# A decoder trunk on one core: the shared filter sum of the convolution moves to ScalarE and GpSimd, and the memory matrices are made in three passes of split float32

## The chip, the core and the metric

The kernel runs on one core of one Trainium2 chip. A core has a matrix engine (TensorE, PE in the profile, with its weight loads shown apart as PEld), a vector engine (VectorE, DVE), an engine for activation functions (ScalarE, ACT), a general engine (GpSimd, POOL), and a queue engine that here issues the transfers (SyncE, SP). Each works through its own list of instructions in order and waits on semaphores for the others. The metric is the device time of one execution in microseconds (us), the median of several executions.

## The reference

The model is a trunk of two layers on 1024 tokens of width 1024, all in float32. The first layer's token mixer is a gated convolution, the second's is forgetting attention. Each layer then attends to 256 memory tokens and ends in an MLP.

```python
def conformer_conv(h, w_pw1, b_pw1, w_dw, b_dw, ln_g, ln_b, w_pw2, b_pw2):
    u = h @ w_pw1 + b_pw1
    a, gate = jnp.split(u, 2, axis=-1)
    u = a * jax.nn.sigmoid(gate)
    u = depthwise_conv(u, w_dw, width 31, causal) + b_dw
    u = jax.nn.silu(layernorm(u, ln_g, ln_b))
    return u @ w_pw2 + b_pw2

def memory_cross_attention(h, mem_n, w_q, w_k, w_v, w_o):
    q, k, v = h @ w_q, mem_n @ w_k, mem_n @ w_v        # 4 heads of 256
    p = softmax(q k^T / sqrt(256))
    return (p v) @ w_o
```

Only the convolution and the preparation for the cross-attention matter here. `mem_n` is the root-mean-square norm of the memory, with a gain per layer.

## The kernel before

Activations lie transposed: 8 chunks of 128 features on the partitions, 1024 tokens along the free side, in two halves of 512 (`X`, `HALVES`). A product in full precision is made of three fast passes: an operand is split into a high part (`act.copy` into the type float32r) and a low part (the rest, `low`, a subtraction), and `passes` multiplies low by high, high by low and high by high. `product` runs these passes into one PSUM bank. An operand that comes as one plain float32 tile is multiplied in one float32 product instead; the profile shows each such product as two matmul instructions.

**The convolution layer** (`conv_layer`). For each chunk m, `gated_unit` makes both halves of `u`: two products of 24 passes each per half, a sigmoid on ScalarE, and one VectorE instruction (L370) that writes `u`. `convolve` then runs the filter of 31 taps over `u`. It uses a trick that halves the work of even and odd output positions: tokens are kept as an even row and an odd row, and

- `both` is a sum over the odd row with the sums of neighbouring taps (`sums`), shared by the even and the odd outputs: 16 steps (L396, then L400 fifteen times);
- `d0` and `d1` are differences of the two rows (L393, L394);
- the even outputs are `both` plus 16 taps on `d0`, the odd outputs `both` plus 15 taps on `d1` (L408). Two accumulators, the two halves of `X`, are built at once; in the built program their instructions alternate.

L354 adds each chunk's result to a running sum for the layer norm. When all 8 chunks are done, `layer_norm` normalizes the halves (L314, L183, L317, L318), and `linear` multiplies by `pw2` (384 passes, results written by L324).

**The memory preparation** (`memory_matrices`) does not depend on the tokens. For each layer and each of 4 heads it makes the keys `kt` and values `vt` of the memory, and from them two matrices that go to DRAM for the attention (`mqk`, `mvo`). It is a generator: four steps to a head, 32 in all, and `conv_layer` calls some of them between its own pieces (`next(prep)`), so that TensorE has work while VectorE runs the filter. In plain float32 it needs 128 products with 256 columns for keys and values a layer, 64 for `mqk`, and 32 with 512 columns for `mvo`.

The order of the instructions on each engine is set when the program is built, by the scheduler of the Tile framework: it works by the order of the code, by priorities and by its own estimate of what is ready. On the chip nothing overtakes. The pool `nrm` has a ring of four buffers under the tag `t`, which squares, the filter's intermediate tiles and others take in the order of the code; whoever takes a buffer waits until the fourth one before has been read.

Of the kernel before, what the change touches and what calls it, by code (L numbers as in the profile page):

```python
# [12 lines left out]
F32 = mybir.dt.float32  # L13
F32R = mybir.dt.float32r
# [72 lines left out]
def trunk(ctx, tc, a, out):  # L87
# [16 lines left out]
    def col(name, i):  # L104
        return par[:, COLS[name] + i : COLS[name] + i + 1]
# [80 lines left out]
    def add_squares(acc, ch):  # L186

        sq = nrm.tile([P, HALF], F32, name="sq", tag="t", bufs=4)
        act.activation(sq, ch, AF.Square)
        if acc is None:  # L190
            return sq
        dve.tensor_tensor(acc, acc, sq, op=ALU.add)
        return acc
# [98 lines left out]

    def conv_layer(pm, prep):
        with tc.tile_pool(name="conv", bufs=2) as cp:
# [44 lines left out]
            for m in range(NCH):  # L339
                if m:  # L340
                    u = padded()
                    for sl in HALVES:
                        gated_unit(pm, cp, m, ahead, hs, u[:, :, PAD // 2 :], sl)
                if m + 1 < NCH:
                    ahead = gate_weights(m + 1)
                for _ in range(2):
                    next(prep, None)

                convolve(cp, m, u, pairs[:, m])
                for s, sl in enumerate(HALVES):  # L350
                    if m == 0:
                        act.copy(acc[s], X[:, m, sl])
                    else:
                        dve.tensor_tensor(acc[s], acc[s], X[:, m, sl], op=ALU.add)  # L354
# [30 lines left out]

    def convolve(cp, m, u, sums):


        n, k = S // 2, TAPS // 2
        even, odd = u[:, 0, :], u[:, 1, :]  # L390
        d0 = cp.tile([P, n + k], F32, name="d0")
        d1 = cp.tile([P, n + k - 1], F32, name="d1")
        dve.tensor_tensor(d0, even[:, : n + k], odd[:, : n + k], op=ALU.subtract)  # L393
        dve.tensor_tensor(d1, even[:, 1 : n + k], odd[:, : n + k - 1], op=ALU.subtract)  # L394
        both = cp.tile([P, n], F32, name="both")
        dve.tensor_scalar(  # L396
            both, odd[:, :n], sums[:, 0:1], col("dw_b", m), op0=ALU.mult, op1=ALU.add
        )
        for j in range(1, k + 1):
            dve.scalar_tensor_tensor(  # L400
                both, odd[:, j : j + n], sums[:, j : j + 1], both, op0=ALU.mult, op1=ALU.add
            )
        out = [X[:, m, sl] for sl in HALVES]
        for s, d, taps in ((0, d0, k + 1), (1, d1, k)):
            y = both
            for j in range(taps):
                w = col("dw_w", m * TAPS + 2 * j + s)
                dve.scalar_tensor_tensor(  # L408
                    out[s], d[:, j : j + n], w, y, op0=ALU.mult, op1=ALU.add
                )  # L410
                y = out[s]

# [20 lines left out]
    def memory_matrices(pp, pq, layer):  # L433
# [3 lines left out]

        def get(src):
            raw = pp.tile([P, NCH, P], F32, name="praw", bufs=3)
            nc.sync.dma_start(raw, src)  # L440
            return raw

        mem = pp.tile([P, NCH, MEM], F32, name="mem", bufs=1)
        nc.sync.dma_start(mem, a["memT"])
        if layer == 0:
            r = inverse_rms([mem[:, c, :] for c in range(NCH)], RMS_EPS)
            rt = const.tile([P, MEM // P], F32, name="mem_r")
            rs = const.tile([P, MEM], F32, name="mem_rs")
            mem_r.extend((rt, rs))
        for c in range(NCH):  # L450
            act.activation(mem[:, c, :], mem[:, c, :], AF.Copy, scale=col(f"src{layer}", c))
        for h in range(MEM_HEADS):
            kv = []
            for w, n in ((wk, "kt"), (wv, "vt")):
                t = bank(pq).rearrange("p (c m) -> p c m", c=2)
                for c in range(2):
                    x = get(w[2 * h + c])
                    product(t[:, c, :], [((x[:, k, :],), (mem[:, k, :],)) for k in range(NCH)])
                o = pp.tile([P, 2, MEM], F32, name=n, bufs=1)
                if w is wk:  # L460
# [3 lines left out]
                    rb = mem_r[1].unsqueeze(1).to_broadcast([P, 2, MEM])  # L464
                    with tc.high_priority(offset=SMALL_FIRST):
                        dve.tensor_tensor(o, t, rb, op=ALU.mult)
                else:
                    act.copy(o, t)
                kv.append(o)
                yield  # L470
            kt, vt = kv
            for j in range(2):

                x = get(wq[h, j])
                for g in range(2):
                    t = bank(pq).rearrange("p (f m) -> p f m", f=2)
                    o = pp.tile([P, 4, P], F32, name="o").rearrange("p (f b) n -> p f (b n)", f=2)
                    for f in range(2):
                        product(t[:, f, :], [
                            ((x[:, 4 * c + 2 * g + f, :],), (kt[:, c, :],)) for c in range(2)  # L480
                        ])
# [6 lines left out]
            for j in range(2):  # L488

                x = get(wo[h, j])  # L490
                for mc in range(2):
                    t = bank(pq)
                    product(t, [
                        (
                            (vt[:, c, mc * P : (mc + 1) * P],),
                            (x[:, 4 * c : 4 * c + 4, :].rearrange("p b n -> p (b n)"),),
                        )
# [864 lines left out]

    with prep_pools(4) as pools, banks(2) as pm:
        conv_layer(pm, chain(*(memory_matrices(*pools, l) for l in range(2))))
    sums = mem_attention(0)
# [80 lines left out]
```

## Time and profile before

| | us |
|---|---|
| median of 3 runs | 2822.2 (2816.68 to 2823.24) |
| the profiled execution's own time | 2825.31 |
| its span, first to last instruction | 2823.3 |
| convolution layer: up to the last write of L324 | 526 |
| of it, the eight filters | 77 to 388 |

The page lists busy time of each engine over the whole span. Lines are those of the kernel before. A duration in it is that of one instruction with its pipeline; where instructions follow each other closely, the distance between two starts is shorter than the duration, and a group's busy time (its union) divided by its count shows that distance. A matmul of 512 columns for example is listed with 391 ns, and 5424 of them fill 1242.4 us, 229 ns each.

### The profile page before, as it was taken

How to read it: one execution, taken by the hardware profiler on the slowest of the kernel's cores; microseconds unless marked ns; L12 is line 12 of the kernel's file. 1: busy time of each engine (PE TensorE's matmuls, PEld its weight loads, DVE VectorE, ACT ScalarE, POOL GpSimd, SP SyncE). 2: the span in 40 equal slices, each digit the busy share in tenths (PEclk: the TensorE clock that was granted, in tenths of full speed). 3: DMA queues.
4: the chain of work that ended last, by engine and by line, in shares of the span. 5: the costliest groups of instructions: out<-in, count | busy, mean ns of one | idle time of the engine just before them, and what ended most of it. 6: DMA issues, size and time to landing. Idle time of an engine off the chain costs nothing.

```text
span 2823.3 us, 36214 instructions
## 1 busy us (share of the span) xinstructions
PE 2740.8 (97%) x12968; PEld 2261.3 (80%) x12968; DVE 2030.9 (72%) x3358; ACT 1278.3 (45%) x2293; POOL 703.1 (25%) x473
## 2 busy tenths in 40 slices
PE   8999999999999999999899999989999999989998
PEld 6777777888888877888688888878888788878886
DVE  5999984555776576777788888875546855577776
ACT  5212143433555553333466666673423655543332
POOL 0000000000065625774000000000000365525773
PEclk9999999999999999999899999999999999999999
DMA  6334364322165585652222221243213455655651
GB/s 219 120 119 135 114 206 124 101 90 70 65 230 177 178 309 187 227 199 89 69 68 70 57 65 55 69 136 98 94 64 105 149 176 190 218 208 197 227 201 61
DMA packets 165428, 390.68 MB, mean 138 GB/s; under 512 B 17264, under 2 KB 46192, under 8 KB 164992
## 3 DMA queue, kind: packets, MB, share of 16 engines
q1 hardware_dynamic: 165248, 388.37, 40.9%
q8 instruction: 102, 1.67, 0.2%
q14 instruction: 78, 0.64, 0.1%
HBM read 270.79 MB, written 113.31 MB: 136 GB/s over the span
## 4 chain that ended last, share of the span: by engine, by line
PE 74%; DVE 12%; ACT 5%; DMA 5%; issue 3%; POOL 1%; SPq 0%; DVEq 0%; POOLq 0%; ACTq 0%
PE mm L1070 34%; PE mm L269 29%; PE mm L1255 5%; DVE w L148 2%; DVE op L148 2%; DVE x L408 1%; PE mm L1341 1%; DVE x L1310 1%; DMA ua<-x 1%; ACT x L1315 1%; PE mm L1353 1%; PE mm L1354 1%; DVE both L400 1%; DVE wl L148 1%; ACT pth L151 1%
## 5 line engine op out<-in xcount | busy, mean ns | idle before, releaser
L1070 PE MATMUL mm<-op,w 128*128 128x512 f32 x5424 | 1242.4, 391 | 24.5 <-ACT m L955 8.7
L1070 PEld LDWEIGHTS mm<-op,w 128*128 128x128 f32 x5424 | 1020.5, 189 | 243.2 <-ACT m L955 9.6
L269 PE MATMUL mm<-op,wh 128*128 128x512 f32 x1056 | 330.5, 394 | 4.2 <-DVE op L148 4.2
L148 DVE TENSOR_TENSOR w<-r,w 128x512 fp32r<-128x512 f32 x264 | 262.6, 998 | 30.5 <-ACT w L653 30.5
L653 ACT CAST w<-r 128x512 fp32r<-128x512 f32 x264 | 163.3, 622 | 262.0 <-PE mm L1070 233.2
L269 PEld LDWEIGHTS mm<-op,wh 128*128 128x128 f32 x1056 | 200.2, 190 | 48.5 <-DVE op L148 6.5
L1255 PE MATMUL mm<-op,wh 128*128 128x512 f32 x736 | 231.4, 396 | 0.0
L148 DVE TENSOR_TENSOR w<-t,w 128x512 fp32r<-128x512 f32 x180 | 178.2, 1005 | 63.2 <-ACT w L653 63.1
L269 PE MATMUL mm<-op,wl 128*128 128x512 f32 x528 | 210.5, 400 | 7.1 <-DVE wl L148 6.2
L207 POOL TENSOR_TENSOR r<-v,mhalf 128x4 f32<-128x4 f32 (+1 forms) x15 | 16.8, 1117 | 741.0 <-DVE v L205 741.0
L647 POOL TENSOR_TENSOR t<-r,t 128x512 f32<-128x512 f32 x104 | 174.9, 1681 | 91.4 <-DVE w L148 54.2
L653 ACT CAST w<-t 128x512 fp32r<-128x512 f32 x180 | 112.0, 622 | 169.8 <-PE mm L1070 140.6
L151 ACT CAST wh<-raw 128x1024 fp32r<-128x1024 f32 x96 | 100.7, 1050 | 193.8 <-PE mm L269 97.5
L865 POOL TENSOR_TENSOR x<-x,x 128x512 f32<-128x512 f32 x112 | 160.2, 1455 | 112.6 <-ACT x L878 101.6
L967 DVE TENSOR_TENSOR x<-mm,x 128x512 f32<-128x512 f32 x160 | 109.5, 684 | 91.1 <-PE mm L1070 73.7
L1255 PEld LDWEIGHTS mm<-op,wh 128*128 128x128 f32 x736 | 139.2, 189 | 26.7
L269 PE MATMUL mm<-op,xsh 128*128 128x512 f32 x512 | 158.0, 393 | 0.0
L1255 PE MATMUL mm<-op,wl 128*128 128x512 f32 x368 | 155.0, 421 | 1.9 <-ACT q L1275 1.9
L151 ACT CAST pth<-mm 128x512 fp32r<-128x512 f32 (+1 forms) x224 | 105.9, 495 | 108.5 <-PE mm L556 80.8
L408 DVE SCALAR_TENSOR_TENSOR x<-d,par,x 128x512 f32<-128x512 f32 x232 | 154.5, 746 | 0.0
L647 POOL TENSOR_TENSOR t<-r,r 128x512 f32<-128x512 f32 x52 | 80.2, 1542 | 295.1 <-DMA r<-in_ff_w 191.0
L1315 ACT ACTIVATE x<-x,nb 128x128 f32<-128x128 f32 (+7 forms) x128 | 99.5, 778 | 109.3 <-DVE nb L1313 100.0
(188 smaller groups left out, 4689.6 us busy)
## 6 DMA issues: line engine op xcount, KB each, us to landing
r<-in_ff_w SPq DMA_DIRECT2D x128, 512.0 KB, 4.0
op<-ua SPq DMA_DIRECT2D x80, 512.0 KB, 6.8
us<-x SPq DMA_DIRECT2D x128, 256.0 KB, 2.9
op<-us SPq DMA_DIRECT2D x64, 512.0 KB, 5.6
raw<-mvo SPq DMA_DIRECT2D x32, 512.0 KB, 3.4
ua<-ul SPq DMA_DIRECT2D x64, 256.0 KB, 2.2
ua<-uh SPq DMA_DIRECT2D x60, 256.0 KB, 2.3
raw<-in_pw SPq DMA_DIRECT2D x24, 512.0 KB, 4.7
```

The lines of the kernel that those rows point to most:

```text
L148: dve.tensor_tensor(lo, src, hi.bitcast(F32), op=ALU.subtract)
L151: act.copy(hi, src)
L269: pe.matmul(out_ps, x, y, start=i == 0, stop=i == len(terms) - 1)
L400: dve.scalar_tensor_tensor(both, odd[:, j : j + n], sums[:, j : j + 1], both, op0=ALU.mult, op1=ALU.add)
L408: dve.scalar_tensor_tensor(out[s], d[:, j : j + n], w, y, op0=ALU.mult, op1=ALU.add)
L647: (dve if g in (2, 3, UP, UP + 1) else pool).tensor_tensor(t, raws[g, x], raws[g, y], op=ALU.subtract)
L653: act.copy(highs[n][0], raws[steps[n][:2]])
L865: eng.tensor_tensor(u[g, x], y1, y2, op=op_)
L967: dve.tensor_tensor(v, sums[key], v, op=ALU.add)
L1070: pe.matmul(sums[key], y, z, start=first and i == 0, stop=n == last_of[key] and i == len(terms) - 1, skip_group_check=True,)
L1255: pe.matmul(t, x, y, start=n == 0, stop=n == len(terms) - 1)
L1315: act.activation(x[:, :n], x[:, :n], AF.Exp, bias=nb, accum_out=rs)
```

## The change

`both` is no longer made on VectorE. ScalarE multiplies the odd row by each tap (`tap`, L397 of the changed kernel; the first step, L394, writes `both` and adds the bias), and GpSimd adds the 15 products to `both`, one after the other (L398). VectorE keeps the differences (now L401, L402) and the 31 taps (L409), which now accumulate in one PSUM bank, `acc`, instead of in the two halves of `X`: first all of `d0`, then all of `d1`. `d0` and `d1` have one buffer each instead of two.

The memory preparation takes split operands. Weights come in halves of 4 chunks; ScalarE makes the high part (`ph`, L448), GpSimd the low part (`pl`, L449), three buffers each. The memory, the keys and the values are split too (`memh`, `meml`, `kth`, `ktl`, `vth`, `vtl`), their low parts on VectorE (L462, L148). The keys' full form is now a tile of the ring `t`. The preparation's PSUM pool goes from 4 banks to 3.

```diff
+        both = cp.tile([P, n], F32, name="both")
+        act.activation(both, odd[:, :n], AF.Identity, scale=sums[:, 0:1], bias=col("dw_b", m))
+        for j in range(1, k + 1):
+            t = nrm.tile([P, HALF], F32, name="tap", tag="t", bufs=4)
+            act.activation(t, odd[:, j : j + n], AF.Copy, scale=sums[:, j : j + 1])
+            pool.tensor_tensor(both, both, t, op=ALU.add)
+        d0 = cp.tile([P, n + k], F32, name="d0", bufs=1)
+        d1 = cp.tile([P, n + k - 1], F32, name="d1", bufs=1)
...
-        both = cp.tile([P, n], F32, name="both")
-        dve.tensor_scalar(
-            both, odd[:, :n], sums[:, 0:1], col("dw_b", m), op0=ALU.mult, op1=ALU.add
-        )
-        for j in range(1, k + 1):
-            dve.scalar_tensor_tensor(
-                both, odd[:, j : j + n], sums[:, j : j + 1], both, op0=ALU.mult, op1=ALU.add
-            )
-        out = [X[:, m, sl] for sl in HALVES]
+        acc = bank(pc)
         for s, d, taps in ((0, d0, k + 1), (1, d1, k)):
             y = both
             for j in range(taps):
+                o = X[:, m, HALVES[s]] if j == taps - 1 else acc
                 w = col("dw_w", m * TAPS + 2 * j + s)
-                dve.scalar_tensor_tensor(
-                    out[s], d[:, j : j + n], w, y, op0=ALU.mult, op1=ALU.add
-                )
-                y = out[s]
+                dve.scalar_tensor_tensor(o, d[:, j : j + n], w, y, op0=ALU.mult, op1=ALU.add)
+                y = acc
...
+        def half(src):
+            raw = pp.tile([P, NCH // 2, P], F32, name="praw", bufs=3)
+            nc.sync.dma_start(raw.rearrange("p k n -> p (k n)"), src.rearrange("p k n -> p (k n)"))
+            return raw
+
         def get(src):
-            raw = pp.tile([P, NCH, P], F32, name="praw", bufs=3)
-            nc.sync.dma_start(raw, src)
-            return raw
...
+            halves = []
+            for i in range(2):
+                raw = half(src[:, 4 * i : 4 * i + 4, :])
+                hi, lo = (pp.tile([P, NCH // 2, P], F32R, name=f"p{x}", bufs=3) for x in "hl")
+                act.copy(hi, raw)
+                pool.tensor_tensor(lo, raw, hi.bitcast(F32), op=ALU.subtract)
+                halves.append((hi, lo))
+            return halves
...
-                    product(t[:, c, :], [((x[:, k, :],), (mem[:, k, :],)) for k in range(NCH)])
-                o = pp.tile([P, 2, MEM], F32, name=n, bufs=1)
+                    product(t[:, c, :], [
+                        ([y[:, k % 4, :] for y in x[k // 4]], (memh[:, k, :], meml[:, k, :])) for k in range(NCH)
+                    ])
+                hi, lo = (pp.tile([P, 2, MEM], F32R, name=n + y, bufs=1) for y in "hl")
...
                     with tc.high_priority(offset=SMALL_FIRST):
+                        o = nrm.tile([P, HALF], F32, name="kt", tag="t", bufs=4)
+                        o = o.rearrange("p (c m) -> p c m", c=2)
                         dve.tensor_tensor(o, t, rb, op=ALU.mult)
+                        split(hi, lo, o)
                 else:
-                    act.copy(o, t)
-                kv.append(o)
+                    split(hi, lo, t)
+                kv.append((hi, lo))
...
-    with prep_pools(4) as pools, banks(2) as pm:
-        conv_layer(pm, chain(*(memory_matrices(*pools, l) for l in range(2))))
+    with prep_pools(3) as pools, banks(2) as pm, banks(1) as pc:
+        conv_layer(pm, pc, chain(*(memory_matrices(*pools, l) for l in range(2))))
```

The products for `mqk` and `mvo` and the squares of the memory change in the same way and are left out here.

What the build makes of it stands at three places. The first is VectorE around the start of the second chunk's filter. Before, this is how it goes from the first chunk to the second: both writes of `u` (L370) stand ahead of all work on their chunk.

```order
L408 SCALAR_TENSOR_TENSOR x_77<-d_624,par,x_77 128x512
L370 SCALAR_TENSOR_TENSOR u<-mm,par,sg 128x2x256 x2
L148 TENSOR_TENSOR wl<-raw,wh 128x1024 x2
L393 TENSOR_TENSOR d_866<-u 128x527
L394 TENSOR_TENSOR d_867<-u 128x526
L396 TENSOR_SCALAR both<-u,sums,par 128x512
L400 SCALAR_TENSOR_TENSOR both<-u,sums,both 128x512 x15
L408 SCALAR_TENSOR_TENSOR x_79<-d_866,par,both 128x512
L408 SCALAR_TENSOR_TENSOR x_80<-d_867,par,both 128x512
L408 SCALAR_TENSOR_TENSOR x_79<-d_866,par,x_79 128x512
```

In the changed program, from the end of the first chunk's filter through the first taps of the second:

```order
L409 SCALAR_TENSOR_TENSOR x_78<-d_999,par,mm 128x512
L402 TENSOR_TENSOR d_1360<-u 128x526
L409 SCALAR_TENSOR_TENSOR mm<-d_1359,par,both 128x512
L409 SCALAR_TENSOR_TENSOR mm<-d_1359,par,mm 128x512 x2
L370 SCALAR_TENSOR_TENSOR u<-mm,par,sg 128x2x256
L409 SCALAR_TENSOR_TENSOR mm<-d_1359,par,mm 128x512 x8
L148 TENSOR_TENSOR wl<-raw,wh 128x1024
L409 SCALAR_TENSOR_TENSOR mm<-d_1359,par,mm 128x512 x3
L370 SCALAR_TENSOR_TENSOR u<-mm,par,sg 128x2x256
L409 SCALAR_TENSOR_TENSOR mm<-d_1359,par,mm 128x512
```

The two writes of the third chunk's `u` now stand 3 and 14 taps deep in the second chunk's filter, whose first tap reads `both`. It is the same at every chunk: the second L370 comes behind 18, 14, 15, 15, 16, 12 and 13 taps of the chunk before it.

The second place is GpSimd in the convolution layer. Before, it has nothing there but small powers for the norms and the clearing of eight paddings (two of the four powers in the fourth row and the last row are already the next stage's):

```order
L207 TENSOR_TENSOR r<-v,mhalf 128x2
L207 TENSOR_TENSOR r<-v,mhalf 128x4 x2
L301 MEMSET u 128x2x15 x6
L207 TENSOR_TENSOR r<-v,mhalf 128x4 x4
L207 TENSOR_TENSOR rf<-v,mhalf 128x4
```

Now it has 120 additions and 128 low parts, mixed. These rows are those of the first two chunks:

```order
L398 TENSOR_TENSOR both<-both,tap 128x512 x13
L301 MEMSET u 128x2x15
L449 TENSOR_TENSOR pl<-praw,ph 128x512 x5
L398 TENSOR_TENSOR both<-both,tap 128x512 x5
L449 TENSOR_TENSOR pl<-praw,ph 128x512
L398 TENSOR_TENSOR both<-both,tap 128x512
L449 TENSOR_TENSOR pl<-praw,ph 128x512 x2
L398 TENSOR_TENSOR both<-both,tap 128x512 x9
L301 MEMSET u 128x2x15
```

Each chunk's 15 additions share the queue with low parts of the weights. 80 of the 128 low parts stand ahead of the end of the last chunk's additions, 48 behind.

The third place is the layer norm behind the filters. On TensorE, before, the norm's small matmuls (L158 and L167) stand between the preparation's products with the seventh head's keys `kt` (its keys and values are the first row):

```order
L269 MATMUL mm<-mem,praw 128x256 x32
L269 MATMUL mm<-kt,praw 128x256 x4
L158 MATMUL mm<-mean_col,acc_564 128x1 x4
L269 MATMUL mm<-kt,praw 128x256
L167 MATMUL mm<-ident,nm 128x128 x4
L269 MATMUL mm<-kt,praw 128x256 x7
L269 MATMUL mm<-praw,vt 128x512 x2
```

Now only the sixth head's keys and values are through by then, and nothing stands between the norm's matmuls until the products with that head's keys (`kth`, `ktl`):

```order
L269 MATMUL mm<-memh,ph 128x256
L158 MATMUL mm<-mean_col,acc_781 128x1 x4
L167 MATMUL mm<-ident,nm 128x128 x4
L158 MATMUL mm<-mean_col,acc 128x1 x4
L167 MATMUL mm<-ident,r 128x128 x4
L158 MATMUL mm<-mean_col,acc_782 128x1 x4
L167 MATMUL mm<-ident,nm 128x128 x4
L269 MATMUL mm<-kth,pl 128x256 x3
```

On VectorE that head's `kt` and its low part stand behind the second half's squares, which use the ring `t` ahead of it:

```order
L314 TENSOR_TENSOR x_92<-x_92,mm 128x512
L183 TENSOR_TENSOR acc<-acc,t 128x512 x5
L489 TENSOR_TENSOR kt<-mm,mem_rs 128x512
L183 TENSOR_TENSOR acc<-acc,t 128x512 x2
L148 TENSOR_TENSOR ktl<-kt,kth 128x512
L205 TENSOR_SCALAR v<-mm 128x4
```

Behind the norm's first sums TensorE has left, in order: the sixth head's products for `mqk` and `mvo`, all of the last two heads, and `pw2`: 192 passes with `memh` or `meml` and 144 with `kth` or `ktl` (256 columns each), 72 with `vth` or `vtl` and the 384 of `pw2` (512 columns each).

35 lines of the change are left out of this document (21 added, 14 removed).

## The prediction

> **What bounds the kernel now.** I read the page first, then busy time by stage, then the lines of the convolution layer, then the chain of waits inside it. The page's first part shows a kernel that TensorE fills:
>
> ```profile
> PE 2740.8 (97%) x12968; PEld 2261.3 (80%) x12968; DVE 2030.9 (72%) x3358; ACT 1278.3 (45%) x2293; POOL 703.1 (25%) x473
> ```
>
> The change touches only the convolution layer, so I cut that into the start, the filters, the layer norm and `pw2`. Columns are PE, PEld, DVE, ACT, POOL busy us with counts, granted clock, share of the DMA engines, GB/s:
>
> ```profile
> 0.00:77.00 77.00, 63.62 (x254) 49.19 (x255) 40.51 (x69) 38.68 (x69) 3.54 (x11) 0.96 0.61 207
> 77.00:388.00 311.00, 306.89 (x1298) 243.49 (x1298) 305.60 (x440) 63.08 (x105) 0.75 (x6) 1.00 0.42 136
> 388.00:431.00 43.00, 41.68 (x201) 32.01 (x199) 31.63 (x54) 27.98 (x51) 2.01 (x2) 1.00 0.61 187
> 431.00:526.00 95.00, 95.00 (x409) 76.30 (x408) 40.40 (x54) 32.14 (x49) 0.00 (x0) 1.00 0.33 99
> ```
>
> In the second row TensorE and VectorE are both full, and ScalarE and GpSimd nearly idle: the change moves work from the full engines to the idle ones. In the third row TensorE stays full during the norm, because preparation is left to do. The single lines give landmarks (least, median, greatest duration, first and last start):
>
> ```profile
> L393 DVE TENSOR_TENSOR d<-u x8: 696/704/709, 76.7 to 351.3; 128x527 f32<-128x527 f32 x8
> L354 DVE TENSOR_TENSOR acc<-acc,x x14: 678/686/695, 150.3 to 388.3; 128x512 f32<-128x512 f32 x14
> L324 DVE SCALAR_TENSOR_TENSOR x<-mm,par,x x16: 745/751/752, 446.9 to 525.5; 128x512 f32<-128x512 f32 x16
> ```
>
> A chunk takes (351.3 - 76.7) / 7 = 39.2 us, the last filter is summed at 389, and `pw2` ends at 526.2, 137 us later. The chain of waits (start, length, what) runs through VectorE there:
>
> ```profile
> 274.25 0.62 DVE d L393
> ...
> 276.77 0.76 DVE both L400
> 277.56 0.76 DVE both L400
> ...
> 288.33 14.00 DVE x L408 x21
> ```
>
> Two distances are to be read here: a step of `both`, which waits for its own predecessor, comes every 0.787 us, and the taps, whose two accumulators alternate, every 14.00 / 21 = 0.667 us.
>
> **Part by part: what gets shorter.** The groups of the stage (busy us, mean ns; idle before):
>
> ```profile
> L400 DVE SCALAR_TENSOR_TENSOR both<-u,sums,both 128x512 f32<-128x512 f32 x120 | 90.2, 752 | 4.1
> L370 DVE SCALAR_TENSOR_TENSOR u<-mm,par,sg 128x512 f32<-128x512 f32 x16 | 11.6, 747 | 2.9 <-PE mm L269 2.9
> L148 DVE TENSOR_TENSOR wl<-raw,wh 128x1024 fp32r<-128x1024 f32 x24 | 28.7, 1220 | 12.5 <-ACT wh L151 12.1 <-DMA x<-in_xT 0.4
> L269 PE MATMUL mm<-mem,praw 128*128 128x256 f32 x512 | 116.7, 386 | 9.1 <-ACT mem L451 8.7 <-DMA praw<-in_mem_wk 0.5
> L269 PE MATMUL mm<-kt,praw 128*128 128x256 f32 x256 | 61.2, 385 | 6.0 <-ACT o L483 4.5 <-DMA praw<-in_mem_wq 1.4
> L269 PE MATMUL mm<-praw,vt 128*128 128x512 f32 x128 | 59.1, 594 | 0.0
> L1070 PE MATMUL mm<-op,w 128*128 128x512 f32 x5424 | 1242.4, 391 | 24.5 <-ACT m L955 8.7 <-DVE x L967 7.6 <-DVE x L814 4.7
> ```
>
> TensorE: the preparation costs 116.7 + 61.2 + 59.1 = 237.0 us. A fast pass of 512 columns costs 1242.4 / 5424 = 0.229. One of 256 columns occurs later in the kernel, in an unbroken run; its first row and a row 47 passes on:
>
> ```profile
> 574.67 0.36 PE L269 MATMUL mm<-pth,wl 128*128 128x256 f32 x1
> ...
> 580.38 0.28 PE L269 MATMUL mm<-pth,wh 128*128 128x256 f32 x1
> ```
>
> That is 5.71 / 47 = 0.121. The change issues 768 + 384 such passes and 192 of 512: 139 + 44 = 183 us, a saving of 54.
>
> VectorE: it loses the 128 steps of `both`, 99 us. But its 248 taps now run in one accumulator, each waiting for the one before, as L400 did. The step is then 0.787 and not 0.667, 30 us back; that the accumulator lies in PSUM no row shows, and I bound it by 0.667 below and by 0.9 above (the wait of L400 again on top). The low parts of keys, values and memory add some 19 us (16 instructions of 128x512 at 0.69, 16 of half the size). VectorE falls from 39 us a chunk to about 33.
>
> **What gets longer.** GpSimd gets 120 additions and 128 low parts, all 128x512. ScalarE gets 128 tap products and 128 casts. Their prices (first the least, median and greatest duration of independent operations, then two that depend on each other with VectorE quiet, then ScalarE by form):
>
> ```profile
> L647 POOL TENSOR_TENSOR t<-r,r x52: 1286/1301/2285, 789.4 to 2754.4; 128x512 f32<-128x512 f32 x52
> ...
> 1097.37 1.29 POOL L647 TENSOR_TENSOR t<-r,r 128x512 f32<-128x512 f32 x1 [20.35 <-DMA r<-in_ff_w]
> 1098.73 1.30 POOL L647 TENSOR_TENSOR t<-r,t 128x512 f32<-128x512 f32 x1
> ...
> L451 ACT ACTIVATE mem<-mem,par 128x256 f32<-128x256 f32 x16 | 6.7, 494 | 2.8 <-DMA mem<-in_memT 2.8
> L182 ACT ACTIVATE t<-mem 128x256 f32<-128x256 f32 x7 | 2.5, 404 | 0.1
> L182 ACT ACTIVATE t<-x 128x512 f32<-128x512 f32 x35 | 20.5, 625 | 8.7 <-DVE acc L183 4.3 <-DVE x L324 4.3
> ```
>
> An addition that waits for the last one costs 1.36, a low part 1.30: 120 x 1.36 + 128 x 1.30 = 330 us of GpSimd. A tap product with its scale from a column is 0.625 + (0.494 - 0.404) = 0.715. ScalarE comes to 162 + 92 + 80 + 10 = 344 us in a stage of over 500, and is covered. No engine's sum exceeds the 526 us there are; by sums alone the layer would shorten.
>
> By the order it does not. VectorE's first tap of chunk m waits for the last addition of `both`. The second write of the next chunk's `u` stands 14.7 taps behind that first tap, on the mean of the seven counts given with the change. And the next chunk's additions need that `u`. So each chunk closes a ring through three engines, whatever TensorE does:
> - VectorE, first tap to `u`: 14.7 x 0.787 + two L370 at 0.75 + one `wl` at 1.22, and the eight low parts of the second layer's memory once, 0.4 a chunk: 14.7 us.
> - ScalarE, first step of `both` and first product: 1.4.
> - GpSimd, to the end of `both`: 15 additions, and 5 low parts among or just ahead of them (between the additions 2 to 5; where there are 2, three more wait for casts that ScalarE does behind its first step): 15 x 1.36 + 5 x 1.30 = 26.9.
> - GpSimd while VectorE works: 2.0, from these rows.
>
> ```profile
> L865 POOL TENSOR_TENSOR x<-x,x x112: 1282/1305/1821, 771.9 to 2459.5; 128x512 f32<-128x512 f32 x112
> L865 POOL TENSOR_TENSOR x<-x,x 128x512 f32<-128x512 f32 x112 | 160.2, 1455 | 112.6 <-ACT x L878 101.6
> L148 DVE TENSOR_TENSOR w<-r,w 128x512 fp32r<-128x512 f32 x264 | 262.6, 998 | 30.5 <-ACT w L653 30.5
> L148 DVE TENSOR_TENSOR op<-x,op 128x512 fp32r<-128x512 f32 x80 | 51.4, 687 | 2.5 <-ACT op L151 1.8 <-ACT op L730 0.6
> L967 DVE TENSOR_TENSOR x<-mm,x 128x512 f32<-128x512 f32 x160 | 109.5, 684 | 91.1 <-PE mm L1070 73.7 <-POOL x L924 17.3
> ```
>
> The MLP has GpSimd and VectorE at work together. There GpSimd's operation grows from 1.282 to 1.455 on the mean, and VectorE's subtraction of two SBUF tiles from 0.687 to 0.998, while the one with a PSUM operand (L967) stays at 0.684. In the changed filter most VectorE operations have a PSUM operand, so I take 0.1 for each of 20 GpSimd operations; the ends are 0 and 5.4 (all two-tile work of the stretch at its own length: `wl` 1.22 and six more of 0.69).
>
> The Trainium skill has a rule on this ("SBUF — State Buffer", section "SBUF: two separate sides"): GpSimd and a VectorE instruction with two SBUF inputs take a shared pair of ports as an exclusive lock for the whole instruction, and the loser waits. The two L148 rows and L967 agree with it in kind. By the rule the upper end, 5.4, would hold, and the sum below would gain 7 x 3.4 = 24 us.
>
> The ring takes 14.7 + 1.4 + 26.9 + 2.0 = 45.0 us a chunk against 39.2. TensorE needs (768 x 0.229 + 183) / 8 = 45 with all the preparation, and (176 + 183 x 5/8) / 8 = 36 with the five heads that stand inside the ring, so it is not what closes it. Behind the waiting tap on VectorE stand the two L370 and the weights' low parts: TensorE's gate products wait for the banks that L370 empties, and fall behind with it.
>
> Transfers: 64 loads of 512 KB become 128 of 256 KB in SyncE's queue, and each waits until GpSimd has read a buffer; stores of `mqk` and `mvo` stand behind them. ScalarE waits for such stores now (total us, times, longest):
>
> ```profile
> ACT o L501 <- DMA mqk<-o: 25.0, 9, 5.1
> ```
>
> I cost this at nothing, since ScalarE may run four products ahead of GpSimd, 5.4 us; where a store is later than that, the additions starve by the difference, up to some 2 us a chunk, which the upper end holds.
>
> **The sum.** The first `u` is there at 79 (76.7 now; GpSimd's first low parts stand ahead of the norms' powers, some 3 us). `both` of chunk 0 ends at 79 + 30.3 = 109, of chunk 7 at 109 + 7 x 45.0 = 424. Sixteen taps and L354 end the first half's sum at 438 (388.3 + 0.7 now). Then the norm: now 42 us from the sum to the second half's last squares and their spread (389 to 431); with 14 taps of the other half mixed in, mostly into its waits, I take 45. The next head's `kt` waits for the ring `t`, so TensorE has only the norm's sums until 438 + 45. What is left then is 336 x 0.121 + 456 x 0.229 = 145 us, and I add 5 for waits between keys and their products. `pw2` ends at 438 + 45 + 150 = 633, where it ends at 526 now: 107 later. Behind it nothing is changed. The profiled execution, 2825.3, becomes 2932; the median of the runs stands 3.1 below it, so 2929.
>
> The ends: with taps at 0.667, 17 GpSimd operations at 1.30 and no lock, a chunk takes 12.9 + 1.4 + 22.1 = 36.4, the sum ends at 367, and with 180 behind it at 547: 21 later, 2843. With a tap at 0.9 and the lock at 5.4 it is 50, the first `u` at 85, and 205 behind: about 690, 2986.
>
> **Rivals.**
> - *TensorE is the bound and the ring does not close* (faster). For it: 306.89 of 311 us busy, and both full engines are relieved. Then the saving of 54 us shows: 2768. Against it: the order of L370. It decides from a chunk of 30 us or less ((526 - 195 - 13 - 109) / 7), far below the ring's own lower end.
> - *GpSimd's rate alone* (no change). If `u` were always early, its 178 operations from the first to the last addition would take 178 x 1.34 = 239 us, the filters would end at 79 + 239 + 13 = 331, and `pw2` at 526: 2822.
> - *The lock at full length* (slower still): 2950 to 2990. For it: the greatest L647, 2.285, is one whole VectorE operation longer than the least. Against it: few such operations.
> - *The ring no slower than now, only the norm's gap* (slower by less): chunks of 37 to 40 us, 2845 to 2890. For it: a tap in PSUM may overlap after all.
>
> **How the numbers follow.** My forecast (2890 to 2950) gets 0.52, the full lock 0.17, the short ring 0.17, GpSimd's rate 0.07, the free TensorE 0.07. The range from 2845 to 2990 leaves out the last two and something at both ends. About 0.3%, 8.5 us, is what a measurement of this kernel can tell from no change: faster 0.08, same 0.06, slower 0.86.
>
> **What would show it.** Right: starts of the differences some 45 us apart; VectorE idle before its first tap of each chunk, waiting for GpSimd's addition; taps at 0.787; TensorE nearly idle for some 40 us of the norm; L324's last start at about 632. Wrong: TensorE at 98% through the filters, or VectorE's wait before the first tap under 1 us, or the sixth head's `kt` ahead of the norm's end.

## The result, and the profile after

The changed kernel takes 2979.6 us (median of 4 runs, 2978.1 to 2986.0) where the kernel before takes 2822.3: the ratio is 1.0566, with a 95% interval from 1.0546 to 1.0587. It is slower by 157 us; forecast were 107. The profiled execution of the changed kernel took 2986.0, 6 above the median of its runs.

The page's first part, and the granted clock of TensorE in 40 slices:

```profile
PE 2765.9 (93%) x13416; PEld 2300.7 (77%) x13416; DVE 2006.9 (67%) x3262; ACT 1437.8 (48%) x2557; POOL 1038.3 (35%) x721
...
PEclk9999976999999999999999999999999999999999
```

TensorE's share fell from 97% to 93%, and its clock sags in the sixth and seventh slice (373 to 522 us), which hold the end of the filters and the norm. The stretches of that layer (columns as in the prediction), cut at the first `u`, the first half's sum, the sixth head's keys, the last head's last product and the end of `pw2`:

```profile
0.00:88.00 88.00, 59.54 (x314) 51.15 (x315) 50.20 (x79) 48.72 (x89) 30.62 (x30) 0.94 0.56 181
88.00:453.00 365.00, 294.58 (x1429) 242.79 (x1428) 257.31 (x312) 178.22 (x294) 260.13 (x196) 0.90 0.32 97
453.00:500.00 47.00, 10.37 (x54) 9.45 (x52) 39.76 (x65) 22.92 (x36) 4.69 (x4) 0.56 0.07 22
500.00:590.00 90.00, 76.26 (x441) 62.91 (x442) 20.35 (x30) 47.73 (x84) 44.70 (x35) 0.94 0.55 164
590.00:677.00 87.00, 84.18 (x373) 68.52 (x372) 28.75 (x36) 24.34 (x36) 3.77 (x3) 1.00 0.34 102
```

In the filters no engine is full any more: TensorE works 295 of 365 us, VectorE 257, GpSimd 260. In the norm TensorE works 10 of 47 us, at a clock of 0.56. The landmarks (least, median, greatest duration in ns, first and last start in us):

```profile
L401 DVE TENSOR_TENSOR d<-u x8: 707/1122/1387, 87.9 to 412.6; 128x527 f32<-128x527 f32 x8
L354 DVE TENSOR_TENSOR acc<-acc,x x14: 678/894/1791, 181.9 to 471.8; 128x512 f32<-128x512 f32 x14
L398 POOL TENSOR_TENSOR both<-both,tap x120: 1260/1292/1927, 93.8 to 436.9; 128x512 f32<-128x512 f32 x120
L489 DVE TENSOR_TENSOR kt<-mm,mem_rs x8: 676/691/692, 25.7 to 573.8; 128x512 f32<-128x512 f32 x8
L324 DVE SCALAR_TENSOR_TENSOR x<-mm,par,x x16: 744/751/752, 578.4 to 675.4; 128x512 f32<-128x512 f32 x16
```

`both` ends at 117.5 for the first chunk and at 438.1 for the last: (438.1 - 117.5) / 7 = 45.8 us a chunk. The first half's last L354 starts at 452.5, the sixth head's `kt` at 499.4, and `pw2` ends at 676.2, 150 us later than before. The chain of waits on GpSimd and VectorE shows one whole ring, from the end of one chunk's `both` at 164.2 to the next at 209.2 (start, length, what; in brackets the idle time before it and its releaser):

```profile
164.24 4.22 POOL L449 TENSOR_TENSOR pl<-praw,ph 128x512 fp32r<-128x512 f32 x3
179.98 4.87 POOL L449 TENSOR_TENSOR pl<-praw,ph 128x512 fp32r<-128x512 f32 x3 [11.52 <-ACT ph L448]
184.81 3.13 POOL L398 TENSOR_TENSOR both<-both,tap 128x512 f32<-128x512 f32 x2
187.90 2.97 POOL L449 TENSOR_TENSOR pl<-praw,ph 128x512 fp32r<-128x512 f32 x2
190.82 18.37 POOL L398 TENSOR_TENSOR both<-both,tap 128x512 f32<-128x512 f32 x13
```

```profile
164.25 1.82 DVE L409 SCALAR_TENSOR_TENSOR mm<-d,par,both 128x512 f32<-128x512 f32 x1 [15.87 <-POOL both L398]
...
168.23 6.29 DVE L409 SCALAR_TENSOR_TENSOR mm<-d,par,mm 128x512 f32<-128x512 f32 x8
...
177.80 0.74 DVE L370 SCALAR_TENSOR_TENSOR u<-mm,par,sg 128x512 f32<-128x512 f32 x1
...
198.52 0.75 DVE L409 SCALAR_TENSOR_TENSOR x<-d,par,mm 128x512 f32<-128x512 f32 x1
...
209.23 1.77 DVE L409 SCALAR_TENSOR_TENSOR mm<-d,par,both 128x512 f32<-128x512 f32 x1 [6.59 <-POOL both L398]
```

VectorE starts its taps when `both` is there, and starts the second write of `u` 13.6 us later. Until then GpSimd has three low parts to do and is otherwise idle: what it waits for are casts (L448) that ScalarE does behind its first step of the next `both`, and that step reads `u`. Then come the 15 additions with five low parts ahead of and among them, while VectorE ends its taps at 199.3 and then waits. So each engine waits for the other once in every chunk. From 80 to 480 us the waits of the two add up as follows (us in total, times, longest; in four chunks GpSimd waits for the first product and in the others for such a cast):

```profile
DVE mm L409 <- POOL both L398: 86.3, 8, 15.9
POOL pl L449 <- ACT ph L448: 66.0, 15, 15.2
...
POOL both L398 <- ACT tap L397: 38.9, 4, 14.0
```

### The profile page after: what moved, and what is told of

The parts are those of the page before. It is cut to its first block, busy times and chain, and to the rows that moved or that the text cites. A ratio compares the mean times of both kernels' runs of the same rounds, so it can differ in the third digit from the quotient of the medians.

```text
span 2983.8 us, 37890 instructions
## 1 busy us (share of the span) xinstructions
PE 2765.9 (93%) x13416; PEld 2300.7 (77%) x13416; DVE 2006.9 (67%) x3262; ACT 1437.8 (48%) x2557; POOL 1038.3 (35%) x721
## 4 chain that ended last, share of the span: by engine, by line
PE 62%; DVE 8%; ACT 5%; DMA 3%; issue 3%; POOL 1%; SPq 0%; DVEq 0%; POOLq 0%; ACTq 0%
PE mm L1094 34%; PE mm L269 17%; PE mm L1279 5%; DVE w L148 1%; DVE op L148 1%; PE mm L1365 1%; DVE x L1334 1%; PE mm L1377 1%; PE mm L1378 1%; ACT x L1339 1%; PE mm L1329 1%; DMA r<-in_ff_w 1%; ACT pth L151 1%; PE mm L1330 1%; ACT wh L151 1%
## 5 line engine op out<-in xcount | busy, mean ns | idle before, releaser
L269 PE MATMUL mm<-op,wh 128*128 128x512 f32 x1056 | 338.3, 401 | 4.7 <-DVE op L148 4.7
L148 DVE TENSOR_TENSOR w<-r,w 128x512 fp32r<-128x512 f32 x264 | 264.2, 1004 | 30.6 <-ACT w L677 30.6
L269 PE MATMUL mm<-op,wl 128*128 128x512 f32 x528 | 212.1, 403 | 26.9 <-DVE u L370 14.1
L1279 PE MATMUL mm<-op,wh 128*128 128x512 f32 x736 | 230.3, 394 | 0.0
L449 POOL TENSOR_TENSOR pl<-praw,ph 128x512 fp32r<-128x512 f32 x128 | 178.2, 1410 | 139.1 <-ACT ph L448 134.4
L148 DVE TENSOR_TENSOR w<-t,w 128x512 fp32r<-128x512 f32 x180 | 177.2, 998 | 66.9 <-ACT w L677 66.7
L398 POOL TENSOR_TENSOR both<-both,tap 128x512 f32<-128x512 f32 x120 | 160.2, 1335 | 46.6 <-ACT tap L397 38.9
L409 DVE SCALAR_TENSOR_TENSOR mm<-d,par,mm 128x512 f32<-128x512 f32 x216 | 162.7, 753 | 5.4
```

Of the source, the lines that this page charges most:

```text
L148: dve.tensor_tensor(lo, src, hi.bitcast(F32), op=ALU.subtract)
L269: pe.matmul(out_ps, x, y, start=i == 0, stop=i == len(terms) - 1)
L398: pool.tensor_tensor(both, both, t, op=ALU.add)
L409: dve.scalar_tensor_tensor(o, d[:, j : j + n], w, y, op0=ALU.mult, op1=ALU.add)
L449: pool.tensor_tensor(lo, raw, hi.bitcast(F32), op=ALU.subtract)
L1279: pe.matmul(t, x, y, start=n == 0, stop=n == len(terms) - 1)
```

## Experiments

Twelve further kernels were run. "Chunk" is the mean distance between the ends of `both` of the first and the last chunk, over 7 (for e2, between the first and the last start of L393); the ratio is to the kernel before, in brackets its 95% interval.

| kernel | us | ratio | chunk | `pw2` ends |
|---|---|---|---|---|
| changed | 2979.6 | 1.0566 [1.0546, 1.0587] | 45.8 | 676 |
| e1 filter's sum alone | 2908.9 | 1.0319 [1.0298, 1.0341] | 46.0 | 609 |
| e2 preparation alone | 3024.0 | 1.0722 [1.0699, 1.0746] | 54.3 (L393) | 722 |
| e3 `u` first | 2956.5 | 1.0488 [1.0469, 1.0506] | 40.3 | 647 |
| e4 `u` first, own tile for `kt` | 2930.1 | 1.0395 [1.0377, 1.0412] | 41.1 | 625 |
| e5 taps' sums in SBUF | 3073.9 | 1.0878 [1.0859, 1.0896] | 56.7 | 762 |
| e6 = e4, two PSUM sums | 2949.7 | 1.0438 [1.0422, 1.0454] | 41.6 | 644 |
| e7 = e4, low parts on VectorE | 2919.1 | 1.0329 [1.0300, 1.0358] | 39.3 | 606 |
| e8 = e6, every second low part on VectorE | 2926.8 | 1.0364 [1.0346, 1.0381] | 39.7 | 623 |
| e9 last three heads' low parts on VectorE | 2972.6 | 1.0529 [1.0508, 1.0551] | 45.9 | 671 |
| e10 first head's low parts on VectorE | 2980.8 | 1.0559 [1.0536, 1.0583] | 45.7 | 673 |
| e11 = e4, both of these | 2922.4 | 1.0356 [1.0335, 1.0378] | 40.4 | 615 |
| e12 = e1, `u` first | 2852.7 | 1.0106 [1.0089, 1.0123] | 36.5 | 558 |

**The two halves apart (e1, e2).** e1 is the changed kernel with the old `memory_matrices`, e2 the old kernel with the new one. Each program has its own line numbers: the additions to `both` are L398 in the changed kernel and L401 where `u` comes first, and L354 is L361 there.

> The filter's sum on ScalarE and GpSimd as changed, the memory preparation as before (float32, no low parts at all). Ring theory: in this order the second write of the next chunk's u stands 25.3 taps behind the first tap (mean of the seven counts), so a chunk takes 25.3 x 0.787 + two L370 and one wl 2.7 + ScalarE 1.4 + 15 additions x 1.36 = 20.4, about 44.5 us, against 39.2 before; first u at 77, last both at 100 + 7 x 44.5 = 411, first half's sum 425, and a tail of about 150 to 165 (two heads of float32 preparation and pw2): 2875 to 2890. Rival, the GpSimd work of the preparation makes the loss: no low parts, so the time stays at 2822 within 10. Rival, GpSimd's own rate: 15 x 1.36 = 20 us a chunk, far below TensorE's need, again 2822.

The ring came: 46.0 us a chunk. GpSimd does no low part in e1 and is idle for more than half of the stretch from 73 to 433 us, yet both waits of the ring stand there:

```profile
POOL both L398 <- ACT tap L397: 201.0, 8, 29.4
DVE mm L409 <- POOL both L398: 116.1, 8, 17.4
```

So a chunk this long needs neither the low parts nor GpSimd's rate. It follows from the order: fewer operations stand on GpSimd's side than in the changed kernel, more taps on VectorE's. The time is 19 us above the range: the first half's sum came at 431 and not at 425, and from there to the end of `pw2` it took 177 us and not 150 to 165.

> The preparation in three passes with GpSimd's low parts as changed, the filter's sum on VectorE as before. Tail theory: the filters lose little (first u at 88, a chunk at 39.2 to 41 since VectorE was full and gets low parts of keys and values: first half's sum at 405 to 415), but three heads stand behind the norm as in the changed kernel, whose 224 us from the first half's sum to the end of pw2 come again: pw2 ends at 630 to 640, 2925 to 2940. Rival, only the ring through GpSimd costs: TensorE's saving shows in the tail, 137 less some 15, 2810 to 2840.

Both theories missed: 3024, 84 above the range of the higher one. The filters stretched to 54.3 us a chunk, though VectorE does there nearly what it did before. First, GpSimd's clearing of the next `u` waits for the last step of `both`, which reads the buffer, and the low parts are queued behind it (waits from 88 to 506 us):

```profile
POOL u L301 <- DVE both L400: 71.3, 6, 17.9
```

Second, low parts that run beside the taps take up to 17.4 us (least, median, greatest duration in ns, then one such place on GpSimd and what VectorE does there, from the timeline):

```profile
L450 POOL TENSOR_TENSOR pl<-praw,ph x128: 1256/1292/17361, 16.1 to 642.5; 128x512 fp32r<-128x512 f32 x128
```

```profile
213.87 16.63 POOL L450 TENSOR_TENSOR pl<-praw,ph 128x512 fp32r<-128x512 f32 x2 [8.40 <-ACT ph L449]
```

```profile
206.66 19.30 DVE L408 SCALAR_TENSOR_TENSOR x<-d,par,x 128x512 f32<-128x512 f32 x29
```

The first of these two low parts took 14.4 us and ended at 228.3, about one operation's length behind the end of the run of taps and the two L354 that follow it (227.2). Five low parts took 13.6 to 17.4, one in each of five chunks, and TensorE's products stood behind them.

**The lock with the sums in SBUF (e5).** The changed kernel with the taps summed in SBUF. The build's order changes with it, and both forecasts count that in:

```
-        acc = bank(pc)
...
-            y = both
+            y, acc = both, X[:, m, HALVES[s]]
```

> The changed kernel with the taps' running sums in SBUF (in X, two alternating, as before the change) and not in one PSUM bank; in the order that follows, all 31 taps stand ahead of the next chunk's second write of u, and 4 to 10 low parts between the chunks' additions. Full-lock theory: GpSimd gets nothing done while VectorE runs 31 taps on SBUF operands without a pause (20.7 us), so single low parts last up to some 20 us, and the low parts pile up ahead of the additions: a chunk takes 20.7 + 3 + 1.4 + 15 x 1.36 + 8 x 1.36 = 56 us against 45.8, the time 3050 to 3070. Rival, GpSimd goes on at about 1.4 us an operation beside the taps: 20.7 + 3 + 1.4 + 20.4 + 2 = 47.5 us a chunk, 2990.

56.7 us a chunk and 3073.9, 4 above the range of the full lock and far from its rival. Here too a low part beside the taps takes up to 13.7 us:

```profile
L448 POOL TENSOR_TENSOR pl<-praw,ph x128: 1257/1290/13722, 15.9 to 682.3; 128x512 fp32r<-128x512 f32 x128
```

**Breaking the ring (e3, e12).** The gates of the next chunk are emitted ahead of this chunk's taps, and the first tap is tied behind the second write of `u` in VectorE's order (no semaphore is added). The loads of the gates' weights move a chunk ahead with them:

```
+                        gated_unit(pm, cp, m + 1, ahead, hs, u[:, :, PAD // 2 :], sl)
...
+                if s == j == 0:
+                    tc.add_manual_dep(nc.cur_bb.bb.instructions[-1], last_u, ...)
```

> The changed kernel, with the order alone altered: the next chunk's u is written ahead of this chunk's first tap, so that no chunk's ring runs through its own taps. Ring theory: a chunk falls from 45.8 to what VectorE, TensorE and GpSimd need each (33, 36 and 15 x 1.36 + 10 low parts x 1.39 = 34), about 36: last both at 118 + 7 x 36 = 370, first half's sum 384, tail 224 as it was: 2911, range 2895 to 2930. Rival, GpSimd's rate or its lock with VectorE sets the 45.8: unchanged, 2980.

The ring is gone: `both` is ready 5 to 13 us before the first tap, which now waits for `u`. But the chunk is 40.3 and not 36, and from the first half's sum to the end of `pw2` it is 238 us and not 224, so the time is 2956 and not 2911. TensorE in its turn waits for low parts in GpSimd's queue, but e7 and e8 below show that this is not all that holds the chunk. The step was right; in the chunk it was worth half of what was expected (5.5 us of 9.8), in the time a third (23 of 69).

> The filter's sum on ScalarE and GpSimd, the preparation in float32 as before the change (2909 in the order that closes the ring, chunks of 46.0), now with the next chunk's u written ahead of this chunk's first tap. If the ring is all that the moved sum cost: chunks fall to TensorE's own need, 22 of gates and some 18.5 of preparation, about 40; last u at 73 + 7 x 40 = 353, its sum and taps 22 + 24, the first half's sum at about 400 to 405 and pw2's end at 537 to 550, 2830 to 2850. If GpSimd's and ScalarE's work beside VectorE costs by itself (lock, ports, buffers): chunks stay at 44 to 46 and the time above 2890.

Without low parts the same edit takes the chunk from 46.0 to 36.5, shorter than forecast and than the 39.2 before the change, and the time from 2908.9 to 2852.7, by 56 us; that is 3 above the range. Nearly two thirds of e1's loss of 88 were the ring, and GpSimd's work beside VectorE does not by itself make the chunk longer. TensorE is nearly full again in the filters (e12, 73 to 402 us, then the norm):

```profile
73.00:402.00 329.00, 307.17 (x1267) 239.97 (x1266) 258.73 (x328) 150.12 (x238) 161.35 (x126) 0.97 0.38 123
402.00:450.00 48.00, 41.79 (x182) 31.52 (x181) 31.29 (x53) 32.33 (x54) 2.03 (x2) 0.93 0.41 134
```

What is left against the kernel before lies behind the last `u`, which is there at 329 (350 before). Its sum ends at 352.0, and its two chains of taps run one after the other from 359.6 to 399.5: in the first VectorE waits 8.4 us for TensorE at `kt`, and among the taps of the second stands the first half's norm. The first half's last sum (L361 here) starts at 381.9 and the second half's at 400.2, where both stood at 388 before; and TensorE, 22 us idle in the filters, has that much more to do behind them: it is busy for nearly all of the time from 402 to the end of `pw2` at 558.

**The norm (e4).** e3 with `pp.tile(..., name="kt", bufs=1)` for the scaled keys in place of the ring `t`.

> As the run before it, and the scaled keys get a tile of their own in place of one of the four of the ring that the norm uses. Theory that the ring of four holds the sixth head's keys until the norm's end: two heads go into the norm, TensorE is busy there, the tail falls from 224 by 30 to 46 us: 2865 to 2885. Rival, the low parts' transfers and casts hold the preparation and not the ring of tiles: as the run before, 2911.

26 us gained over e3, a little less than the first theory's 30 to 46. In the 47 us behind the first half's sum TensorE works 38.9 us (436 to 483), where e3 has 24.3 (408 to 455). From that sum to the end of `pw2` it is now 188 us and not 238; but the sum itself comes 28 later, since `kt` now stands among the last taps and VectorE waits there 10.4 us for TensorE. The absolute range was missed, as e3's was, because the filters came to 41 and not 36.

**GpSimd's queue or the taps (e6, e7, e8).** All three start from e4. In e6 the taps have two PSUM banks, `accs[s]`, in place of `acc`, and the preparation one less. In e7 the weights' low parts are made by `low(lo, raw, hi)` on VectorE. e8 has e6's banks and makes the low parts on `(pool if i else dve)`, so every second one on VectorE.

> The kernel with u first and the keys' own tile (2930), with two PSUM banks for the taps' sums in place of one (one bank less for the preparation), so that two chains alternate. If the taps' chain of 0.787 holds the chunks at 41.9: 31 x 0.12 = 3.7 us less a chunk, 2900. If TensorE's waits for GpSimd's low parts hold them (88 us of waits in the filters): 2915 to 2930. Where the taps stay at 0.787 with two banks, an operand in PSUM cannot overlap: 2930 or a little above, for the bank that is missing.

> The kernel with u first and the keys' own tile (2930), with the 128 low parts of the preparation on VectorE in place of GpSimd. If GpSimd's queue, where the low parts stand among the additions, holds TensorE: GpSimd falls to 21 us a chunk, but VectorE gets 10 x 0.69 more and comes to about 41 a chunk, so the filters stay near 41.9 and the tail gains some 15 to 25 us: 2900 to 2915. If it does not hold TensorE, VectorE's extra 88 us show: 2960 or more.

> The kernel with u first and the keys' own tile (2930), with two PSUM banks for the taps and every second low part on VectorE. By the queue theory each engine then has room: VectorE 34, GpSimd 28, TensorE 36 us a chunk, so about 37.5 a chunk and a tail of 150: pw2 ends at about 555, 2850 to 2865. If neither the queue nor the taps hold the chunks (the transfers or the halved TensorE clock do): 2915 to 2930.

e6: where two chains alternate, 14 taps run in 9.31 us, 0.665 each, so a sum in PSUM overlaps as one in SBUF did. The time rose by 20 all the same and lies above all three forecasts: the chunk stayed at 41.6, and `pw2` ended 19 later. The preparation's missing bank may be the cause; it was not tried by itself. e7 gained 11 and missed its range by 4; e8 gained 3 on e4 (23 on e6, from which only the low parts' engine differs) and came out 62 above its forecast, in the range of its rival. So with the taps alternating and GpSimd rid of half its low parts the chunk still stays at 40. In e8 TensorE is the fullest engine of the filters (213.4 of the 240 us from 112 to 352) at a clock of 0.95. What keeps it from 36 these runs don't settle: the transfers, the banks and the clock are left.

**The start and the rest (e9, e10, e11).** The low parts of some heads go to VectorE: `engine = dve if layer and h else pool`, and for the first head `not (layer or h)`.

> The changed kernel (2980), with the low parts of the last three heads, which stand behind the filters, on VectorE in place of GpSimd. Theory that GpSimd's low parts, one after another at 1.3 us and more, set TensorE's pace there (passes of wo at 0.31 to 0.35 us and of wk and wv at 0.15 to 0.16, where 0.23 and 0.12 are seen in unbroken runs): the 177 us from the sixth head's keys to the end of pw2 fall to 155 to 165, the time to 2955 to 2968. Rival, the halved TensorE clock behind the norm, the keys' cast behind the norm's work on ScalarE, or the loads set the pace: 172 to 177, the time 2975 to 2985.

From the sixth head's `kt` to the end of `pw2` it is 166.4 us in place of 176.8: 10 of the 27 that the prediction lacked there. Both missed their forecasts, 166.4 narrowly and 2972.6 by 5. Half of the gain was lost again ahead of it: `kt` itself starts at 504.3, 4.9 later, so `pw2` ends only 5.5 earlier. The low parts of that stretch in the changed kernel, and then in e9:

```profile
L449 POOL TENSOR_TENSOR pl<-praw,ph 128x512 fp32r<-128x512 f32 x37 | 47.5, 1297 | 46.0 <-ACT ph L448 41.8 <-PE mm L269 4.2
```

```profile
L449 DVE TENSOR_TENSOR pl<-praw,ph 128x512 fp32r<-128x512 f32 x37 | 25.1, 691 | 36.7 <-ACT ph L448 36.5 <-PE mm L269 0.2
```

> The changed kernel (2980), with the low parts of the first head alone on VectorE in place of GpSimd. Theory that GpSimd's pace in the first head's low parts, behind which TensorE reaches the first norm's means, makes the first u late: it is there at 75 to 79 and not at 88, and the rest follows as it is: 2967 to 2972. Rival, the 256 KB loads or ScalarE's casts make it late: first u at 86 to 88, 2978 to 2984.

The first `u` came at 82.8, between the two ranges, and nothing of it reached the end: 2980.8, which can't be told from 2979.6. GpSimd has low parts of the second head ahead of and among the first additions, so `both` ended at 115.1 in place of 117.5. In e7, with no low parts on GpSimd at all, the first `u` was there at 74.6 (85.0 in e4, from which e7 starts).

> The kernel with u first and the keys' own tile (2930), with the low parts of the first and of the last three heads on VectorE. If both ends are paced by GpSimd's low parts: 10 less at the start and 10 to 20 less behind the filters, 2900 to 2910. If only the start is: 2918 to 2922. Either way the filters stay near 42 us a chunk, and the time above the kernel before.

2922.4, 8 below e4 and in neither range, nearer to the second.

No version tried beats the kernel before. The nearest is e12, 31 us slower.

## Why the prediction was right or wrong

It was right on the sign and on the ring, and 2979.6 lies within its range of 2845 to 2990; the size was short by 50 us (by 43 at the end of `pw2`). That it lies within the range is in part luck. The time misses the band that was forecast, 2890 to 2950, and falls into that of a rival, the full lock, whose mechanism the trace does not show. The upper end of the range was added up from a chunk of 50, a first `u` at 85 and 205 us behind the first half's sum. The chunk came to 45.8, but the first `u` came at 87.8 and the stretch behind the sum took 223: two of the three terms lay beyond their upper ends, and the ring's room made up for them. The terms one by one:

- *The ring*: right. 45.8 us a chunk for 45.0. From the first tap to `u` it took 15.1 (mean of seven; 14.7 forecast), from `u` to the end of `both` 30.6 (28.3 + 2.0 = 30.3). That it is the order, and not a rate, e1 and e12 show; for the changed kernel itself e3 shows it, with a gain of 5.5 us a chunk. The transfers, which the sum put at nothing, can have cost the ring no more than the 0.8 that it is longer.
- *The tap's step*: right. 8 taps in 6.29 us are 0.786 each, with the sum in PSUM. e6 shows that it is the single chain that costs, not PSUM.
- *GpSimd's 330 us*: 160 + 178 = 338. The sum of its work is no bound, which refutes that rival: GpSimd is idle for 105 us of the filters, and the time is not 2822.
- *TensorE's saving of 54 us*: right in the price of a pass and wrong as a saving. Passes of 256 columns start 0.120 apart (median), but up to the end of `pw2` TensorE is busy for 525 us (the five rows above), against 507 before (63.6 + 306.9 + 41.7 + 95.0). It runs in bits between waits, and around the norm its clock is the lower the less it works; why is not shown here. In the 47 us or so behind the first half's sum it is busy for 10 at a clock of 0.56 in the changed kernel, for 24 at 0.72 in e3, for 39 at 0.89 in e4, and for 42 of 43 at 1.00 before. The low clock lasts into the work behind the norm; these rows show 505 to 510, and 5 us on (the clock is the third number from the end; the matmuls have 256 columns or fewer in the first row and 512 in the second, so their counts don't compare):

```profile
505.00:510.00 5.00, 5.00 (x24) 4.96 (x24) 3.08 (x6) 2.48 (x5) 0.00 (x0) 0.50 0.00 0
510.00:515.00 5.00, 4.88 (x21) 3.33 (x19) 4.38 (x7) 5.00 (x9) 0.00 (x0) 1.00 0.00 0
```

- *The first `u` at 79*: mis-sized. It came at 87.8, 9 late. The term took 3 us for GpSimd's low parts ahead of the norms' powers. But TensorE does all of the first head's keys and values ahead of the norm's means, at the pace of their low parts, and ScalarE squares the first half from 30.8 on (12.7 before), behind casts. e10 gives 5 of the 9 back, e7 all of them.
- *The norm of 45*: right, 46.9 from the first half's sum to the next `kt`. e4 shows the named cause, the ring `t`: with a tile of its own for `kt`, TensorE works through the norm, and 26 us come back against e3.
- *The 150 of the rest*: mis-sized, and the largest miss: 176.8. I had 145 by unbroken passes and 5 for waits. GpSimd's pace in the low parts is 10 of the 27 (e9). The halved clock takes some 3 to 5, an estimate: from 500.8 to 510 some 36 matmuls start 0.213 apart, where passes of 256 columns start 0.120 apart elsewhere (36 x 0.093 = 3.3), and half of those 9 us is the most it can be. The other 12 or so are not isolated; in the trace TensorE waits there 11.8 us for low parts, in 18 short waits, and ScalarE's casts, from which the low parts are made, wait 18 us for loads of weights.
- *Nothing behind `pw2`*: 10 us more came there in the profiled execution (150 at the end of `pw2`, 160.5 at the end), 8 of them in the first MLP, whose instructions are the same. Of these 10 some 3 are the distance of the profiled executions to their medians (6.4 and 3.0). e1 is later by 4 there too and regains it in the second MLP. The clock fits the 8. The two rows below are the same stretch, 224 to 624 us behind the end of `pw2`, in the changed kernel and before. In the changed kernel the clock is halved there in three spells of 13.6 us together (at 950, 1193 and 1227), before in none, and half of 13.6 is 6.8. No run sets the clock alone, so this is not shown:

```profile
900.00:1300.00 400.00, 391.65 (x1699) 322.36 (x1698) 269.58 (x330) 215.77 (x359) 197.37 (x130) 0.98 0.57 199
750.00:1150.00 400.00, 392.50 (x1728) 323.79 (x1728) 276.19 (x336) 214.99 (x358) 209.64 (x136) 1.00 0.57 199
```

- *The full lock* (0.17): for the kernel as changed it did not come. In the filters GpSimd's additions took 1.34 us on the mean and its low parts 1.47, where the median is 1.29. The other side paid: VectorE's operations on two SBUF tiles wait for GpSimd's.

```profile
L402 DVE TENSOR_TENSOR d<-u 128x526 f32<-128x526 f32 x8 | 13.6, 1694 | 0.0
L409 DVE SCALAR_TENSOR_TENSOR mm<-d,par,both 128x512 f32<-128x512 f32 x16 | 21.4, 1339 | 86.5 <-POOL both L398 86.3
L354 DVE TENSOR_TENSOR acc<-acc,x 128x512 f32<-128x512 f32 x13 | 15.6, 1198 | 0.2
L148 DVE TENSOR_TENSOR vtl<-mm,vth 128x512 fp32r<-128x512 f32 x4 | 2.8, 692 | 12.1 <-ACT vth L151 12.1
```

The second difference takes 1.69 in place of 0.70, the first taps 1.34 in place of 0.75 (0.76 in e1, without low parts), the sums 1.20 in place of 0.69; `vtl`, with one operand in PSUM, still 0.69. By their places in the order most of these lie outside the ring, or where VectorE waits for `both` anyway; the first tap lies in it.

## What to carry to other kernels

Moving work from a full engine to an idle one pays only if the results don't go round: before summing loads, follow one tile through all engines in the order in which each queue holds its instructions, and see whether the loop closes (46 us a chunk with GpSimd half idle, 36.5 with the same work in another order). Here that alone was not enough: e12 is still 31 us slower than the kernel before. What the full engine had been hiding shows next, so cost the stages behind the change at the pace of their slowest supplier, not at the pace of an unbroken run. And where GpSimd works beside VectorE, keep the sums that VectorE runs in long chains in PSUM (2980 us here against 3074, where the order changed too).

## What the runs showed of the hardware

In e2 GpSimd was shut out by a whole run of VectorE's instructions, and not by one. A low part that met VectorE's alternating taps on SBUF operands, 0.667 us apart and each started before the last had ended, took 13.6 to 17.4 us in place of 1.29, some 20 instructions. Beside the chain of `both`, also on two SBUF operands but each waiting for the last, low parts came through at 6.48 / 4 = 1.62 us. There both sides paid: VectorE's 11 steps took 15.11 / 11 = 1.37 each and not 0.787 (GpSimd's row of the timeline, then VectorE's):

```profile
412.25 6.48 POOL L450 TENSOR_TENSOR pl<-praw,ph 128x512 fp32r<-128x512 f32 x4 [4.88 <-PE mm L269]
```

```profile
410.18 15.11 DVE L400 SCALAR_TENSOR_TENSOR both<-u,sums,both 128x512 f32<-128x512 f32 x11
```

The Trainium skill ("SBUF — State Buffer", section "Who interferes with whom") says that a VectorE instruction with two SBUF inputs contends with a GpSimd instruction that reads SBUF, and that the one that issues first holds the ports for its whole instruction. The rows agree in kind (with one operand in PSUM, `vtl`, nothing is lost); in e2 and e5 the loser waited for a run of overlapping instructions. That the overlap is what decides is read from these two kinds of rows and was not tried by itself.
